# The output weights' row sums of a hybrid encoder block: three of eight formed in the opening, five spread over the first two pairs of heads

## The chip, the cores and the metric

The kernel runs on one core of one Trainium2 chip. The metric is the device time of one execution in microseconds; the figure given for a kernel is the median of its runs. A profile of one execution lies beside the times. It names the engines PE (TensorE, matmuls), PEld (its weight loads), DVE (VectorE), ACT (ScalarE), POOL (GpSimd) and SP (SyncE, which issues most DMAs).

## The reference

One layer (D = 1024) over 1024 frames with 16 learned meta tokens ahead of them. Four heads of an mLSTM matrix memory and four of multi-scale retention share one input projection; each head's output is normalised, multiplied by a gate, and all of them go through w_out. A gated MLP with a depthwise convolution and a final norm follow. All of it is float32.

```python
proj = up @ w_in                      # q, k, v, o, gates i and f of 4 mLSTM heads; q, k, v, g of 4 retention heads
qk = silu(causal_dwconv(concat(ml_q, ml_k), ml_conv_w))
h_ml = sigmoid(ml_o) * head_norm(mlstm_chunkwise(q, k, v, li, lf), ml_norm_g)
h_rt = silu(rt_g) * head_norm(retention_chunkwise(rotary(rq), rotary(rk), rv), rt_norm_g)
h = h + concat(h_ml, h_rt) @ w_out    # w_out: 2048 x 1024
h = h + (silu(causal_dwconv(u @ w_up, ffn_conv_w)) * (u @ w_gate)) @ w_down
```

## The kernel before

Every float32 product is made of three matmuls on split operands: ScalarE casts a high part ("hi", line 488), VectorE subtracts it to get the low part ("lo", line 494), and TensorE sums hi x hi, hi x lo and lo x hi (lines 948 to 950). The large products are blocked 2 x 2 and take seven block products for eight. These need sums and differences of the blocks, of activations (`usum`, lines 2046 and 2048) and of weights (lines 582 to 589). A projection of one head and kind (`wino_fm`: q and k as "q", the two gate blocks as "o"; `v_steps`: values of a pair) is seven steps over two chunks of tokens, each ended by an eviction from PSUM on ScalarE or VectorE (`evac`, lines 1039 to 1043), which the tiles `raw`, `sig` and `v` take.

**The output product** (`Seven`, from about 500 us on) also needs weight sums. For each k of eight, rows k and k + 8 of w_out (128 x 1024 each) give two combined tiles in DRAM, named `wsw65_k` and `wsw73_k`. They are formed by DMAs alone in `w_sums` (line 662): SP issues three plain copies for a k (line 667: 512 KB and twice 256 KB), and GpSimd then issues four accumulating transfers of 256 KB in three steps (`add`, line 650: two that add other quarters of w_out, then one that adds a half of the 65 tile to its other half, then one that adds that to the 73 tile). Each add has to wait until the transfers before it on the same tile have landed, and GpSimd's queue is in order, so what stands behind an add waits with it. Before the change all eight k are formed in one go in the opening: 24 copies, held until the low parts of the third token range are made (`norm_lows(2)`, line 2015), and 32 adds, step by step over all k. They are read first in the output product at 668.9 us.

**The opening** (lines 1931 to 2090) loads and norms the tokens, projects values, gates and q, k of head 4 (a retention head, handled first), and forms the activations' block sums S1 to S4. SP's loads of weights, of the rotary tables (`A<-rot`, lines 1175 and 1176) and the sums' copies share one queue in program order. From there on `go` writes the work out: the projection's steps in order, and between them pieces of side work, above all the scan of the head before. `scan_a` makes scores `s`, their weighted form `pt` (VectorE, lines 1640 and 1647), its split `ph` and `pl` (GpSimd, lines 1632 and 1651) and the weighted keys `kw` (ScalarE, line 1627); `scan_v` splits the values (`vh`, `vl`, GpSimd, lines 1663 and 1664); `scan_b` uses these on TensorE (`u` and `n`, lines 1670 to 1697). The heads come as 4, then the pairs (0, 1), (2, 3), (5, 6), then 7; a pair is the projections q a, values, o a, q b, o b.

**What sets the order.** `watch` adds up a cost for every instruction as the program is written, so that the writer has a clock per engine and for the DMA wire. A generator that is started by `spawn` is taken up again by `tick` when that clock allows; `lag(8)` lets 8 us of the planned TensorE time pass. Units in the list `units` are started when the projection steps come near them; a unit of size 0 is side work at that place. `RULES` holds seven numbers per projection (lines 48 to 69): how many units ahead pending work may be taken, how long after its planned end a step may follow, two limits on how far VectorE may run behind, the most side tasks in one slot, which of three orders of the queues is used, and how many tasks with TensorE work fit in a slot. `pinned` keeps the order so written on TensorE, VectorE and ScalarE; `last["pace"]` is the latest eviction made by VectorE.

Of the kernel before, what the change touches and what calls it, by code (L numbers as in the profile page):

```python
# [30 lines left out]
HB = 4 * P  # L31
# [15 lines left out]

RULE = (3, 0.5, 3.0, 2.5, 2, 0, 1)
RULES = {
# [39 lines left out]
def body(ctx, tc, h_in, vecs, cst, mask_in, rot, w_v0, w_vp, w_g, w_out, w_up, w_gate, w_down, out):  # L89
    nc = tc.nc  # L90
# [9 lines left out]
    def dep(later, first, sync):  # L100
        kind = mybir.DependencyClass.Sync if sync else mybir.DependencyClass.NoSync
        tc.add_manual_dep(later.ins, first.ins.name, mybir.DependencyInfo(kind, mybir.DependencyReason.DATA), reason="order")
# [4 lines left out]
    last = {}  # L107
# [194 lines left out]
    def unit(key, size, make):  # L302
        units.append((key, size, make))
# [23 lines left out]
    def main_job(nm, *srcs):  # L327
        i = job(nm, *srcs)
        line.append(i)
        return i  # L330
# [61 lines left out]
    def spawn(g, q=pend, key=None):  # L392
        if dealt[0]:
            if next(g, pend) is not pend:
                q.append(g)
                until[id(g)] = fin[0]
                owner[id(g)] = key
        elif held:
            next(g)
            held[0].append(g)  # L400
        else:
            for _ in g:
                pass
# [42 lines left out]
    def lag(us):  # L446
        t = load["PE"]
        while dealt[0] and not rush[0] and load["PE"] - t < us:
            yield
# [24 lines left out]
    class Ready(dict):  # L474
        def add(self, key):
            self[key] = fin[0] + 0.05
# [73 lines left out]
    def u_load(key, *srcs):  # L550
        nm = "_".join(str(k) for k in key)
        i = main_job(nm, *srcs)

        def make():
            r = pairs_of(nm, 2)

            def g():
                yield from jwait(i)
                yield from parts(key, r, jget(i))
                jfree(i)  # L560
            spawn(g(), key=key)
            return r
        unit(key, 2, make)
# [34 lines left out]
    def u_fm(kind, h, *extra):  # L598
        w = w_g[GI[kind, h]]
        nm = f"{kind}{h}"  # L600
        ja = main_job(nm + "a", w[:, HB:3 * HB])
        jb = main_job(nm + "b", w[:, 3 * HB:], w[:, :HB])
        quartered((kind, h), (ja, ja, jb, jb), lambda: [jraw[x][:, i * HB:(i + 1) * HB] if x in jraw else None for x in (ja, jb) for i in (0, 1)], 1, {5: (jb,), 6: (ja,)}, nm)
        for e in extra:
            e()
# [25 lines left out]
    def m_unit(h):  # L631
# [12 lines left out]
            spawn(g())  # L644
        unit(("m", h), 0, make)

    sums = {(g, st_, k): dram.tile([P, 2 * HB], F32, name=f"ws{g}{st_}_{k}") for g, n in (("w", 8), ("d", KD)) for st_ in ("65", "73") for k in range(n)}

    def add(x, y):
# [2 lines left out]
    def wsum(g, k):  # L652
# [6 lines left out]
        add(d73[:, HB:], v11)  # L659
        add(d65[:, :HB], d65[:, HB:])  # L660
        add(d73[:, :HB], d65[:, :HB])

    def w_sums(ks):
        for k in ks:
            d65, d73 = (sums["w", x, k] for x in ("65", "73"))
            for x, y in ((d65, w_out[k]), (d73[:, HB:], w_out[k][:, HB:]), (d73[:, :HB], w_out[k + 8][:, :HB])):
                dep(nc.sync.dma_start(x, y), last["lows", 2], True)
        for step in range(3):
            for k in ks:
                d65, d73 = (sums["w", x, k] for x in ("65", "73"))  # L670
                if step == 0:
                    add(d65[:, HB:], w_out[k + 8][:, HB:])
                    add(d73[:, HB:], w_out[k][:, :HB])
                else:
                    add((d65, d73)[step - 1][:, :HB], (d65[:, HB:], d65[:, :HB])[step - 1])

    dcount = [0]

# [30 lines left out]
    def r_units(*ks):  # L709
        return [lambda k=k: first_right(k) for k in ks]  # L710
# [30 lines left out]
    def v_units(p, s):  # L741
        return [lambda: v_unit(p, s)]

    q4 = w_g[GI["q", 4]]
    u_load(("q4", 0), q4[:, HB:3 * HB])
    u_load(("q4", 1), q4[:, 3 * HB:], q4[:, :HB])

    def m_units(h):
        return [lambda: m_unit(h)]
    u_fm("o", 4, *v_units(0, 0))  # L750
    prev = 4
    for p, (a, b) in enumerate(PAIRS):
        u_fm("q", a)
        u_vp(p)
        u_fm("o", a, *v_units(p, 1), *m_units(prev))
        u_fm("q", b, *(r_units(0, 1) if p == 2 else ()))
        u_fm("o", b, *(v_units(p + 1, 0) if p < 2 else r_units(2, 3)), *m_units(a))
        prev = b
    u_fm("q", 7, *r_units(4, 5))
    u_fm("v", 7, *r_units(6, 7))  # L760
# [1224 lines left out]
    w = [ready["q4", i] for i in range(2)]  # L1985
# [29 lines left out]
    norm_lows(2)  # L2015
    fourth = norm_sums(3, True)
    last["third"] = last["added"]
    w_sums(range(8))
    meta_done()
    for i, x in enumerate(x0):  # L2020
        after(V.tensor_copy(ug[:, 4 * i:4 * i + 4], x[:, :, :META]), last["third"])
# [85 lines left out]
    for p, (a, b) in enumerate(PAIRS):  # L2107
# [38 lines left out]
        prev = b  # L2146
# [14 lines left out]
    for k in range(KW):  # L2161
        if k % 2 == 0:
            x = upool.tile([P, 2 * T], F32R, tag=("uh0", "ul0", "uh1", "ul1")[k // 2], name=f"wone{k}")
        o = (k % 2) * 2 * HB
# [167 lines left out]
    for t, (st, k) in enumerate(mixw.steps):  # L2332
# [4 lines left out]
        if st == "65" and k == 5:  # L2337
            x = fp.tile([P, 4 * XW], F32, name="wm", tag="xl6", bufs=1)
# [243 lines left out]
    for i in range(1, NPAIR):  # L2582
        u, g = up_part(i), gate_part(i)
# [109 lines left out]
    for p in (1, 2):  # L2693
# [5 lines left out]
        else:  # L2699
            for mb in (1, 4):  # L2700
                x = RES[mb][:, OP[2][0]:OP[2][1]]
# [109 lines left out]
```

## Time and profile before

| what | value |
|---|---|
| median of 3 runs | 1505.08 us (1505.03 to 1505.53) |
| the profiled execution | 1503.68 us |
| its span | 1501.9 us |
| mean granted TensorE clock | 0.993 |
| moved by DMA | 223.85 MB, mean 149 GB/s |
| GpSimd's DMAs (queue q0) | 31.46 MB, 11.2% of 16 engines' span |

The span is what the trace covers; the execution's own time is 1.8 us longer. A group of the profile has its line, engine, operation, tile written and tiles read (buffer numbers left out), shape and count. "Idle before" is the time in which an engine stood still just ahead of an instruction, with the event that ended it. In the window rows the granted clock is 1.00 at full speed.

### The profile page before, as it was taken

To read this page: it belongs to the slowest core of one execution; us is meant where nothing else is said; L and a number is where in the kernel's file an instruction comes from. 1 tells how busy PE (TensorE), PEld (TensorE's weight loads), DVE (VectorE), ACT (ScalarE), POOL (GpSimd) and SP (SyncE) were. 2 spreads that over 40 slices of the span, in tenths; PEclk is the share of its full clock that TensorE was granted. 3 is DMA by queue.
4 is the path that set the end of the run, shared out by engine and by line. 5 is a ranking of instruction groups with operands and counts; after the bars stand their busy time and mean duration, and the time that the engine had idled before them with its cause. 6 is when DMAs were issued, how large, how long until landed. Compare 5 with 4: busy or idle time off the path is not lost.

```text
span 1501.9 us, 26232 instructions
## 1 busy us (share of the span) xinstructions
PE 1475.5 (98%) x10032; PEld 1342.3 (89%) x10032; DVE 1092.0 (73%) x2110; ACT 755.8 (50%) x1468; POOL 216.9 (14%) x440
## 2 busy tenths in 40 slices
PE   9988999999999999999999999999999999999997
PEld 7977999999999999987888999888888888888887
DVE  7975876778777677857867887666666666777666
ACT  6554655654655455544454664444444444444443
POOL 1233130314031403040000002222210000000000
PEclk9999999999999999999999999999999999999998
DMA  7993233223312235697333258888762225933213
GB/s 264 277 201 86 85 113 113 86 85 103 123 57 100 71 127 179 201 404 257 106 105 130 96 175 214 214 218 204 185 154 80 73 78 188 351 102 101 99 43 113
DMA packets 98014, 223.85 MB, mean 149 GB/s; under 512 B 10728, under 2 KB 25776, under 8 KB 97584
## 3 DMA queue, kind: packets, MB, share of 16 engines
q1 hardware_dynamic: 78640, 183.29, 36.1%
q0 software_dynamic: 13056, 31.46, 11.2%
q10 hardware_dynamic: 6192, 7.41, 1.4%
q8 instruction: 79, 1.29, 0.4%
q14 instruction: 47, 0.39, 0.1%
HBM read 186.44 MB, written 75.54 MB: 174 GB/s over the span
## 4 chain that ended last, share of the span: by engine, by line
PE 90%; DVE 6%; DMA 2%; ACT 1%; issue 1%; SPq 0%; DVEq 0%; POOL 0%; POOLq 0%; ACTq 0%
PE pdx L950 3%; PE pdx L949 3%; PE pdx L948 3%; PE pup_x L949 3%; PE pup_x L948 3%; PE pup_x L950 3%; PE pga_x L948 2%; PE pga_x L949 2%; PE pga_x L950 2%; PE pdy L950 2%; PE pdy L949 2%; PE pwx L950 2%; PE pdy L948 2%; PE pwx L948 2%; PE pwx L949 2%; PE n L1697 2%
## 5 line engine op out<-in xcount | busy, mean ns | idle before, releaser
L787 ACT CAST hi_up<-raw_up 128x512 fp32r<-128x512 f32 (+1 forms) x52 | 36.4, 719 | 110.1 <-PE pga_z L949 61.1
L788 DVE TENSOR_TENSOR lo_up<-raw_up,hi_up 128x512 fp32r<-128x512 f32 (+1 forms) x52 | 41.4, 810 | 38.3 <-ACT hi_up L787 37.5
L949 PE MATMUL pup_x<-ul_g,hi_up 128*128 128x256 f32 (+1 forms) x240 | 67.4, 282 | 0.0
L948 PE MATMUL pup_x<-uh_g,hi_up 128*128 128x256 f32 (+1 forms) x240 | 67.2, 282 | 0.0
L788 DVE TENSOR_TENSOR lo_ga<-fraw_ga,hi_ga 128x512 fp32r<-128x512 f32 (+1 forms) x51 | 40.6, 800 | 35.7 <-ACT hi_ga L787 35.5
L950 PE MATMUL pup_x<-uh_g,lo_up 128*128 128x256 f32 (+1 forms) x240 | 66.4, 282 | 0.0
L788 DVE TENSOR_TENSOR lo_d<-rd,hi_d 128x1024 fp32r<-128x1024 f32 (+1 forms) x34 | 37.7, 1113 | 32.8 <-ACT hi_d L787 32.7
L950 PE MATMUL pdx<-uh_d,lo_d 128*128 128x512 f32 (+1 forms) x156 | 57.9, 375 | 0.0
L787 ACT CAST hi_ga<-fraw_ga 128x512 fp32r<-128x512 f32 (+1 forms) x51 | 35.4, 712 | 44.5 <-PE pup_z L949 22.6
L949 PE MATMUL pdx<-ul_d,hi_d 128*128 128x512 f32 (+1 forms) x156 | 57.8, 374 | 0.0
L787 ACT CAST hi_d<-rd 128x1024 fp32r<-128x1024 f32 (+1 forms) x34 | 32.3, 959 | 49.1 <-PE pdy L949 32.5
L2678 POOL TENSOR_TENSOR resid<-resid,Rc 128x256 f32<-128x256 f32 x2 | 1.4, 716 | 381.4 <-ACT Rc L858 381.4
L657 POOL DMA_DIRECT2D wsd<-w_down_d x33 | 19.1, 687 | 236.5 <-DVE s2up L2436 232.8
L950 PE MATMUL pdy<-uh_d,lo_d 128*128 128x512 f32 x132 | 51.9, 393 | 0.0
L949 PE MATMUL pdy<-ul_d,hi_d 128*128 128x512 f32 x132 | 51.7, 392 | 0.0
L948 PE MATMUL pdx<-uh_d,hi_d 128*128 128x512 f32 (+1 forms) x156 | 48.5, 372 | 0.0
L948 PE MATMUL pdy<-uh_d,hi_d 128*128 128x512 f32 x132 | 47.9, 389 | 0.0
L1664 POOL TENSOR_TENSOR vl<-v,vh 128x258 fp32r<-128x258 f32 (+1 forms) x48 | 34.7, 723 | 89.2 <-PE n L1671 63.8
L948 PE MATMUL pga_x<-uh_g,hi_ga 128*128 128x512 f32 x120 | 47.5, 396 | 0.0
L949 PE MATMUL pga_x<-ul_g,hi_ga 128*128 128x512 f32 x120 | 47.5, 396 | 0.0
L950 PE MATMUL pga_x<-uh_g,lo_ga 128*128 128x512 f32 x120 | 47.1, 393 | 0.0
L949 PEld LDWEIGHTS pup_x<-ul_g,hi_up 128*128 128x128 f32 x240 | 45.4, 189 | 0.9 <-DVE ul_g L2206 0.2
(1749 smaller groups left out, 6001.1 us busy)
## 6 DMA issues: line engine op xcount, KB each, us to landing
raw_up<-w_up_d SPq DMA_DIRECT2D x22, 512.0 KB
fraw_ga<-w_gate_d SPq DMA_DIRECT2D x22, 512.0 KB
acts<-cv SPq DMA_DIRECT2D x44, 256.0 KB
wsd<-w_down_d POOLq DMA_DIRECT2D x44, 256.0 KB, 6.1
rd<-wsd SPq DMA_DIRECT2D x22, 512.0 KB
raw_m<-w_out_d SPq DMA_DIRECT2D x14, 512.0 KB
raw_vm<-w_vp_d SPq DMA_DIRECT2D x12, 512.0 KB
raw_vp<-w_vp_d SPq DMA_DIRECT2D x12, 512.0 KB
```

The lines of the kernel that those rows point to most:

```text
L657: dep(G.dma_start(x, y), last["pace"], True)
L787: AC.copy(hi[:, o:o + n], x)
L788: V.tensor_tensor(lo[:, o:o + n], x, hi[:, o:o + n].bitcast(F32), ALU.subtract)
L948: m.append(PE.matmul(pt, ah, xh_, start=first and k == 0, stop=False, skip_group_check=True))
L949: PE.matmul(pt, ah, xl_, start=False, stop=False, skip_group_check=True)
L950: m.append(PE.matmul(pt, al, xh_, start=False, stop=last and k == n - 1, skip_group_check=True))
L1664: G.tensor_tensor(low, v, vh.bitcast(F32), ALU.subtract)
L1697: PE.matmul(pn[:L, :nv], qd, state["C"][:, :nv], start=False, stop=True)
L2678: nc.gpsimd.tensor_tensor(RES[mb][:, a0:t1], RES[mb][:, a0:t1], R[1], ALU.mult)
```

## The change

Rows 0 to 2 stay in the opening, with the same copies and adds, but the copies are now held until `last["scale"]`, the scaling of the third token range, which is written before its low parts. Rows 3 to 7 become units of their own (`w_unit`): the three copies are issued when the unit is started, then each of the three steps of adds after another `lag(8)`; every one of these DMAs also waits for the eviction that `last["pace"]` names at that moment. One unit hangs on each of: o of head 0, q and o of head 1 (rows 3, 4, 5), o of head 2, q of head 3 (rows 6, 7). Four entries of `RULES` have new numbers: o of heads 0 and 1, q of heads 1 and 2.

```diff
-    ('o', 0): (4, 0.8, 3.0, 3.0, 4, 0, 1),
-    ('o', 1): (3, 1.2, 2.0, 1.5, 2, 1, 3),
+    ('o', 0): (2, 0.8, 3.0, 3.0, 1, 0, 1),
+    ('o', 1): (3, 1.2, 2.0, 1.5, 2, 1, 1),
...
+    def w_copies(k, gate):
+        d65, d73 = (sums["w", x, k] for x in ("65", "73"))
+        for x, y in ((d65, w_out[k]), (d73[:, HB:], w_out[k][:, HB:]), (d73[:, :HB], w_out[k + 8][:, :HB])):
+            dep(nc.sync.dma_start(x, y), gate, True)
+
+    def w_adds(k, step):
+        d65, d73 = (sums["w", x, k] for x in ("65", "73"))
+        if step == 0:
+            return add(d65[:, HB:], w_out[k + 8][:, HB:]), add(d73[:, HB:], w_out[k][:, :HB])
+        return add((d65, d73)[step - 1][:, :HB], (d65[:, HB:], d65[:, :HB])[step - 1]),
+
+    def w_unit(k):
+        def make():
+            def g():
+                w_copies(k, last["pace"])
+                for step in range(3):
+                    yield from lag(8)
+                    for m in w_adds(k, step):
+                        dep(m, last["pace"], True)
+            spawn(g())
+        unit(("w", k), 0, make)
...
-        u_fm("o", a, *v_units(p, 1), *m_units(prev))
-        u_fm("q", b, *(r_units(0, 1) if p == 2 else ()))
-        u_fm("o", b, *(v_units(p + 1, 0) if p < 2 else r_units(2, 3)), *m_units(a))
+        u_fm("o", a, *v_units(p, 1), *m_units(prev), *w_units(1))
+        u_fm("q", b, *(r_units(0, 1) if p == 2 else ()), *w_units(1))
+        u_fm("o", b, *(v_units(p + 1, 0) if p < 2 else r_units(2, 3)), *m_units(a), *w_units(p < 2))
...
-    w_sums(range(8))
+    for k in range(3):
+        w_copies(k, last["scale"])
+    for step in range(3):
+        for k in range(3):
+            w_adds(k, step)
```

The same instructions are there in both kernels; the change moves them. TensorE's order is the same up to the S1 step of head 0's o projection and again from the S2 step of the second pair's values on (but for a few matmuls of the 73 step of the output product, which stand in another order). Between those the scan of heads 0 and 1 stands one step later or several steps earlier among the projections' steps.

The first place is GpSimd's queue at the end of the opening, before. `wsw65_6` and the like are the sums of row 6, `ph4_1` and `pl4_1` the split scores of head 4's chunk 1.

```order
L650 DMA wsw65_6_165<-wsw65_6_165 128x512
L650 DMA wsw73_3_170<-wsw65_3_162 128x512
L650 DMA wsw65_7_166<-wsw65_7_166 128x512
L650 DMA wsw73_4_171<-wsw65_4_163 128x512
L650 DMA wsw73_5_172<-wsw65_5_164 128x512
L650 DMA wsw73_6_173<-wsw65_6_165 128x512
L650 DMA wsw73_7_174<-wsw65_7_166 128x512
L1113 MEMSET v0_10_1924 128x4x2
L1113 MEMSET v0_00_1727 128x4x2
L1632 CAST ph4_1_1397<-pt4_1_1387 128x128
```

The same place after the change.

```order
L672 DMA wsw73_0_167<-wsw65_0_159 128x512
L672 DMA wsw65_2_161<-wsw65_2_161 128x512
L672 DMA wsw73_1_168<-wsw65_1_160 128x512
L672 DMA wsw73_2_169<-wsw65_2_161 128x512
L1125 MEMSET v0_10_1889 128x4x2
L1125 MEMSET v0_00_1692 128x4x2
L1644 CAST ph4_1_1362<-pt4_1_1352 128x128
```

Twelve adds stand ahead of the cast now, where 32 stood.

The second place is VectorE's order where the rotary tables are first used, before. `uS4l` is a low part of the activations' block sum S4, `A1_4` and `A2_4` are the tables, `qT4` and `kT4` what is made of them.

```order
L1043 TENSOR_TENSOR sig_110<-sig_110,po4y1_976 128x256
L2057 TENSOR_TENSOR uS4l_929<-s4_0_838,uS4h_928 128x1056
L2057 TENSOR_TENSOR uS4l_929<-s4_1_839,uS4h_928 128x1056
L1252 TENSOR_TENSOR qT4_1018<-rawq_102,A1_4_906 128x528
L1253 TENSOR_TENSOR kT4_1019<-kT4_1019,A2_4_907 128x528
```

And after.

```order
L1055 TENSOR_TENSOR sig_110<-sig_110,po4y1_941 128x256
L1264 TENSOR_TENSOR qT4_983<-rawq_102,A1_4_871 128x528
L2073 TENSOR_TENSOR uS4l_894<-s4_0_803,uS4h_893 128x1056
L2073 TENSOR_TENSOR uS4l_894<-s4_1_804,uS4h_893 128x1056
L1265 TENSOR_TENSOR kT4_984<-kT4_984,A2_4_872 128x528
```

The product with the first table now stands ahead of the two splits.

The third place is GpSimd's queue in the scan of head 0, before, around the splits of chunk 6 (`vh0_6`, `ph0_6`, `vl0_6`, `pl0_6`).

```order
L1663 CAST vh0_6_2547<-v0_01_2250 128x258
L1710 COPY den0_2156<-v0_00_1727 128x1
L1632 CAST ph0_6_2559<-pt0_6_2553 128x128
L1664 TENSOR_TENSOR vl0_6_2548<-v0_01_2250,vh0_6_2547 128x258
L1651 TENSOR_TENSOR pl0_6_2560<-pt0_6_2553,ph0_6_2559 128x128
```

And after.

```order
L1675 CAST vh0_6_2529<-v0_01_2215 128x258
L1722 COPY den0_2121<-v0_00_1692 128x1
L672 DMA wsw65_3_162<-w_out_d 128x512
L672 DMA wsw73_3_170<-w_out_d 128x512
L1644 CAST ph0_6_2541<-pt0_6_2535 128x128
L1676 TENSOR_TENSOR vl0_6_2530<-v0_01_2215,vh0_6_2529 128x258
L1663 TENSOR_TENSOR pl0_6_2542<-pt0_6_2535,ph0_6_2541 128x128
```

The first two adds of row 3 stand ahead of the split of chunk 6's scores; the other rows' adds stand in the same way among the splits of heads 0 to 3, the four of row 4 and the four of row 7 each in one piece ahead of the first split of heads 1 and 3. In SP's order, row 3's copies stand between the two loads for head 1's q, row 4's ahead of the first load for head 1's o, row 5's ahead of the first load for head 2's q (`raw_q2a`), and rows 6 and 7 likewise in the second pair.

More of the change, by code (lines that the diff above doesn't have):

```diff
@@ L661, in wsum @@
         add(d73[:, :HB], d65[:, :HB])
[L663 to L675, printed above, removed]
     dcount = [0]
@@ L746, in body, with w_units @@
     u_load(("q4", 1), q4[:, 3 * HB:], q4[:, :HB])
+    wk_ = list(range(3, 8))
+    def w_units(n):
+        return [lambda: wk_ and w_unit(wk_.pop(0))] * n
     def m_units(h):
```

4 rows, old and new, of the table RULES are left out of this document.

## The prediction

> **What bounds the kernel now.** I read the page first (busy shares, the chain of waits), then busy time by stage, then TensorE's own waits, and last the timelines of the two stretches where TensorE stands still.
>
> ```profile
> PE 1475.5 (98%) x10032; PEld 1342.3 (89%) x10032; DVE 1092.0 (73%) x2110; ACT 755.8 (50%) x1468; POOL 216.9 (14%) x440
> 80.00:100.00 20.00, 14.72 (x107) 14.04 (x106) 16.85 (x49) 10.38 (x18) 7.21 (x10) 0.91 0.99 203
> 100.00:120.00 20.00, 14.05 (x107) 12.33 (x106) 11.13 (x29) 9.02 (x23) 7.20 (x10) 0.94 0.98 177
> 140.00:550.00 410.00, 409.72 (x3389) 392.59 (x3389) 302.98 (x698) 230.62 (x482) 89.95 (x223) 1.00 0.29 94
> ```
>
> The window rows give the stretch, its length, busy time of PE, PEld, DVE, ACT and POOL, the granted TensorE clock, the DMA engines' busy share and GB/s. TensorE is busy 98% of the span, so time can only be won where it stands. Of its 26 us idle, 5.3 + 6.0 = 11.2 us lie between 80 and 120 us, where the DMA engines are at 0.98 to 0.99; from 140 to 550 us, where the five moved rows go, it stands 0.28 us and DMA is at 0.29. The first two of its waits make nearly all of the 11.2:
>
> ```profile
> PE n L1670 <- POOL ph L1632: 6.8, 1, 6.8
> PE po4x L948 <- ACT sig L1041: 4.6, 1, 4.6
> PE pz L1879 <- POOL zero L289: 1.3, 1, 1.3
> PE prc L854 <- DVE rcolc L845: 0.6, 1, 0.6
> ```
>
> (Engine, tile and line that waited, its releaser, total us, times, longest. The third comes before the first matmul.) I take the two in turn, with the change's part in each.
>
> **Term 1, the wait of 4.6 us.** TensorE needs an eviction that ScalarE makes late, since ScalarE stands behind a rotary copy that waits for VectorE, and VectorE waits for the rotary tables:
>
> ```profile
> 68.71 0.34 SPq L1175 DMA_DIRECT2D A<-rot_d  x1
> 69.88 13.06 DMA A<-rot_d
> 74.54 2.42 DVE L2057 TENSOR_TENSOR uS4l<-s,uS4h 128x1056 fp32r<-128x1056 f32 x2
> 80.35 0.71 DVE L1252 TENSOR_TENSOR qT<-rawq,A 128x528 f32<-128x528 f32 x1 [3.39 <-DMA A<-rot_d]
> 83.03 0.71 DVE L1253 TENSOR_TENSOR kT<-kT,A 128x528 f32<-128x528 f32 x1 [1.97 <-DMA A<-rot_d]
> 81.15 0.63 ACT L1249 COPY rawq<-rawk 64x528 f32<-64x528 f32 x1 [3.83 <-DVE qT L1252]
> 86.16 0.36 ACT L1041 ACTIVATE sig<-po4x 128x256 f32<-128x256 f32 x1
> 86.57 0.39 PE L948 MATMUL po4x<-uS3h,hi_o 128*128 128x256 f32 x1 [4.64 <-ACT sig L1041]
> 89.62 0.42 PE L948 MATMUL po4y<-uS4h,hi_o 128*128 128x258 f32 x1
> 89.83 0.42 PE L949 MATMUL po4y<-uS4l,hi_o 128*128 128x258 f32 x1
> 93.55 0.28 PE L948 MATMUL po4x<-u22h,hi_o 128*128 128x256 f32 x1
> 93.67 0.28 PE L949 MATMUL po4x<-u22l,hi_o 128*128 128x256 f32 x1
> 254.78 0.62 ACT L488 CAST hi_q<-raw_q2a 128x512 fp32r<-128x512 f32 x1 [0.41 <-DMA raw_q2a<-w_g_d]
> 251.05 0.33 SPq L338 DMA_DIRECT2D raw_q2a<-w_g_d  x1
> ```
>
> The second table took 13.06 us from its issue. A load of nearly the same size in a quiet stretch, raw_q2a, took 254.78 - 251.05 = 3.73 us. The queue is full because of the sums:
>
> ```profile
> 26.43 1.56 DVE x L916 x4
> 32.63 30.92 SPq L667 DMA_DIRECT2D wsw<-w_out_d  x24
> L650 POOL DMA_DIRECT2D wsw<-w_out_d x16: 805/814/960, 37.2 to 95.9; - x16
> L650 POOL DMA_DIRECT2D wsw<-wsw x16: 812/822/837, 49.3 to 120.0; - x16
> DMA to landing us min/median/max: 4.3/7.6/12.0
> ```
>
> The change leaves 9 of 24 copies (8 MB in 30.92 us, so 3 MB in about 11.6) and 12 of 32 adds, and the copies wait for the last scaling in the first row instead of the split that ends at 32.6. From 28.0 us that is copies to 40 and three steps of adds at 4.3 to 7.6 us each, over by 53 to 63 us, before the tables are asked for at 68.7. Those stay where they are: they wait for a buffer. The tables then land at about 72.4 and 75, and VectorE loses neither 3.39 nor 1.97: its work comes 5.36 us earlier. ScalarE's eviction goes from 86.16 to 80.8, before TensorE asks for it at 81.9. The stall of 4.64 goes, and with it the slow matmuls behind it: from 86.57 to about 90.2 they start 0.21 us apart where the pair at 93.55 starts 0.12 apart, 1.65 us lost. TensorE would win 6.3, but the next steps wait for VectorE's sums, which come only 5.36 earlier, so **5.4 us** (bounds 3, if the tables still land late, and 6.3). The order puts the first table product ahead of two splits; by 74.5 (the place of the splits now) its table has landed, so that costs nothing; TensorE comes to those splits only after 81.9, so a table that is some us late is covered too.
>
> **Term 2, the wait of 6.8 us.** The first matmul on chunk 1's split scores waits for GpSimd, whose in-order queue holds the adds, to the last:
>
> ```profile
> 114.15 0.28 PE L1672 MATMUL u<-vh,kl 128*128 128x256 f32 x1
> 111.54 0.40 SPq L338 DMA_DIRECT2D raw_vp<-w_vp_d  x1
> 117.70 1.14 ACT L488 CAST hi_vp<-raw_vp 128x512 fp32r<-128x512 f32 x2 [5.13 <-DMA raw_vp<-w_vp_d]
> 118.75 0.36 ACT L1627 ACTIVATE kw<-s,cs 128x128 fp32r<-128x128 f32 x1
> 119.97 0.82 POOL L650 DMA_DIRECT2D wsw<-wsw  x1 [5.13 <-issue]
> 120.89 0.29 POOL L1632 CAST ph<-pt 128x128 fp32r<-128x128 f32 x1
> 121.24 0.58 PE L1670 MATMUL n<-vh,ph 128*128 128x256 f32 x1 [6.81 <-POOL ph L1632]
> 124.54 0.30 PE L949 MATMUL pq0x<-uS3l,hi_q 128*128 128x264 f32 x1
> ```
>
> With no add behind 63 us GpSimd is free and this cast follows its input at once. The stall goes, and so does a second slow stretch of 3.3 us at half pace (121.24 to 124.54), about 1.65 us: 8.5 us. What is late next is the same cast for chunk 2. It needs kw at 118.75, which stands on ScalarE behind two casts that wait for raw_vp. That load, 5.4 us earlier (106.1) and 3.73 us long, lands at 109.9; the casts end at 111.0, kw at 111.4, the scores' split some 1.3 us later, 112.7. TensorE, 5.4 us earlier and unstalled, comes for it at about 111.7 (114.3 - 5.4, then 1.0 of chunk 1, 1.5 of projection, 0.3 of scores). So 1 us stays (0 to 2.4, the upper end with the 6.1 us that the load took before): **7.5 us**, bounds 6 and 8.5.
>
> The trace has no stall of TensorE between 0.6 and 4.6 us but the 1.3 before its first matmul, so whether this remaining 1 us slows the matmuls after it isn't shown; the nearest row, the 4.64 us, would add 1.65, the 0.6 nothing, and I take the short one, being nearer. The Trainium skill (TensorE: Matmul & The Clock Gate, "What's actually happening") says that the clock halves only after an idle window of about 3.4 us; by it the residue costs no clock and the sum stays, by the long row it would be 1.65 us less.
>
> **Term 3, the five rows in the pairs.** Each adds three copies to SP's queue (median 0.49 us) and four adds of about 0.82 us to GpSimd, which is busy 90 of 410 us there: 20 x 0.82 = 16 us fit. Neither engine is on the path; what counts is who stands behind them. On GpSimd that is the splits of scores and values:
>
> ```profile
> 203.16 0.29 POOL L1632 CAST ph<-pt 128x128 fp32r<-128x128 f32 x1 [2.27 <-DVE pt L1640]
> 205.36 0.47 POOL L1651 TENSOR_TENSOR pl<-pt,ph 128x128 fp32r<-128x128 f32 x1
> 208.51 0.29 PE L1670 MATMUL n<-vh,ph 128*128 128x258 f32 x1
> 213.82 0.29 POOL L1632 CAST ph<-pt 128x128 fp32r<-128x128 f32 x1 [3.11 <-DVE pt L1640]
> L948 PE MATMUL pq2x<-u11h,hi_o x8: 283/285/393, 265.2 to 267.9; 128*128 128x264 f32 x8
> ```
>
> Ahead of the two casts GpSimd stood 2.27 and 3.11 us, and the split of the first ends (205.83) 2.7 us before its matmul: two adds of 1.6 us are covered if their operands have landed. They mostly have: the plan lets 8 us of TensorE's time pass between a row's steps, and the adds here land in 7.6 us at the median in a full queue. On SP a row's megabyte takes 30.92 / 8 = 3.9 us of the queue and stands ahead of a weight load (row 5's ahead of raw_q2a). That load's cast was already 0.41 us late; but TensorE uses it only at 265.2, 10 us later. The copies' and adds' wait for a VectorE eviction holds back the same splits, which wait for later VectorE results anyway. The new order rules alter TensorE's row from head 0's o steps to the first steps of the second value projection, with equal work; the trace cannot price that. I bound term 3 by 0, as all has cover and there is no idle to win (0.28 us), and by 6, one stall like the 4.64 with its slow stretch; nearer the cover: **1.5 us**.
>
> **The sum.** The profiled execution took 1503.68 us, its span 1501.9. 1503.68 - 5.4 - 7.5 + 1.5 = 1492.3. The median of the runs, 1505.08, is 1.4 above that execution, so the forecast is 1493.7. The bounds of the terms: gains of 3 + 6 - 6 = 3 up to 6.3 + 8.5 = 14.8, that is 1502.1 to 1490.3.
>
> **The rivals.**
>
> *Only GpSimd's stall goes (0.13).* The copies start earlier, beside the opening's weight loads, and the tables or VectorE stay as late as now. For it: VectorE is busy 16.85 of 20 us from 80 to 100. Against: 5.36 us of its idle time there name the tables. Gain 7.5 - 1.5 = 6: 1499.
>
> *Loads stand behind copies (0.08).* In the pairs three loads (of q1, o1 and q2) follow a row's copies in SP's order; if each cast holds ScalarE for the 3.9 us and TensorE feels it whole, 11.7 us come back of 12.9: 1503.9, no change. Against it stand the 10 us of raw_q2a. The Trainium skill (DMA: Bandwidth & Descriptors, "Queues, rings and completion order") says that a DMA engine takes the descriptors of one issuing queue in order, which is this mechanism and speaks against the change; the 13.06 us of the table bear it out in a full queue.
>
> *GpSimd blocks the scan (0.10, slower).* An add at the head of GpSimd's queue waits for its transfer, as at 119.97, and the splits behind it stand. If each of five rows held GpSimd for the median landing of 7.6 us with 2.7 of slack, TensorE would stall 4.9 us a row, 24.5 in all: 1505.1 - 12.9 + 24.5 = 1516.7. It turns the sign once a row costs over 12.9 / 5 = 2.6 us, so where GpSimd is held over 5.3 us a row. Against it: the 8 us between steps.
>
> **Chances.** Forecast 0.69, the three rivals 0.13, 0.08 and 0.10. A difference of 0.2%, 3 us, is about what a measurement of this kernel tells from none. Faster by more: the forecast and the first rival, 0.82. Within it: the second, 0.08. Slower: 0.10. The range takes the bounds of the terms and the first rival, widened at the low end by a microsecond for the runs' own spread: 1489 to 1502. It leaves out the second and third rivals.
>
> **What would show it.** Right: the rotary product without a DMA wait and TensorE's wait on that eviction under 1 us; no add later than about 63 us until the pairs; the split for chunk 1 right behind its scores; the projection's matmul that stands at 124.54 now about 12 us earlier; in the pairs at most 2 us of idle. Wrong: tables that still take over 8 us; a wait for the chunk 2 split above 2.4 us; adds in the pairs that hold GpSimd over 5 us with TensorE standing behind them.

## The result, and the profile after

The changed kernel takes 1495.59 us (median of 6 runs, 1493.04 to 1498.06) beside 1505.05 (6 runs, 1502.08 to 1505.53): a ratio of 0.9939, 95% interval 0.9926 to 0.9953, or 9.5 us less. The forecast was 1493.7. The profiled execution took 1498.06 us (span 1496.3), the slowest of the six, so its trace shows only 1498.06 - 1503.68 = -5.6 us; which steps make that can be read from it one by one.

The stages and waits first (windows and TensorE's own waits of the changed kernel, columns as before):

```profile
80.00:100.00 20.00, 18.09 (x146) 17.12 (x145) 17.86 (x53) 12.05 (x24) 0.00 (x0) 1.00 0.09 28
100.00:120.00 20.00, 18.08 (x136) 16.36 (x135) 12.93 (x39) 7.70 (x20) 6.47 (x16) 1.00 0.32 108
140.00:550.00 410.00, 406.21 (x3350) 387.59 (x3349) 306.37 (x689) 227.00 (x476) 111.20 (x237) 1.00 0.43 121
...
PE s L1622 <- DVE kl L1648: 3.5, 2, 1.9
PE pz L1891 <- POOL zero L289: 1.3, 1, 1.3
PE po4x L960 <- DVE sig L1055: 0.8, 1, 0.8
```

Between 80 and 120 us TensorE stands 3.8 us in place of 11.2, at full clock, and the DMA engines are at 0.09 and 0.32 in place of 0.99 and 0.98. Both large waits are gone. But from 140 to 550 us, where it stood 0.28 us, it now stands 3.8.

To price each stretch, five matmuls are looked up in both traces: the time of one before minus its time after is the lead that the changed kernel has there. First the rows of before, then the same matmuls after:

```profile
59.16 0.65 PE L988 MATMUL pv<-w0lo,u22h 128*128 128x264 f32 x4
104.84 0.29 PE L949 MATMUL pq0x<-uS2l,hi_q 128*128 128x264 f32 x1
192.17 0.28 PE L950 MATMUL po0y<-u12h,lo_o 128*128 128x258 f32 x1
331.15 0.28 PE L949 MATMUL pv1y<-lo_vp,uS4h 128*128 128x256 f32 x1
449.95 0.29 PE L950 MATMUL pq5x<-u22h,lo_q 128*128 128x264 f32 x1
```

```profile
60.35 0.65 PE L1000 MATMUL pv<-w0lo,u22h 128*128 128x264 f32 x4
100.73 0.29 PE L961 MATMUL pq0x<-uS2l,hi_q 128*128 128x264 f32 x1
181.28 0.28 PE L962 MATMUL po0y<-u12h,lo_o 128*128 128x258 f32 x1
323.27 0.28 PE L961 MATMUL pv1y<-lo_vp,uS4h 128*128 128x256 f32 x1
444.29 0.29 PE L962 MATMUL pq5x<-u22h,lo_q 128*128 128x264 f32 x1
```

The lead is -1.19, 4.11, 10.89, 7.88 and 5.66 us. So the opening loses 1.2, the stretch of the rotary tables wins 5.3, the stretch of the first scan wins 6.8, and the pairs give back 3.0 and then 2.2, 5.2 together. After that nothing changes (5.62 at the end).

The two places of the gain, as the timelines of GpSimd, SP, VectorE, ScalarE and TensorE have them (start, duration, instruction, idle time before it and its cause):

```profile
59.76 0.83 POOL L672 DMA_DIRECT2D wsw<-wsw  x1 [2.55 <-DMA wsw<-wsw]
69.29 0.34 SPq L1187 DMA_DIRECT2D A<-rot_d  x1
75.12 0.70 DVE L1264 TENSOR_TENSOR qT<-rawq,A 128x528 f32<-128x528 f32 x1
82.06 0.36 ACT L1053 ACTIVATE sig<-po4x 128x256 f32<-128x256 f32 x1
108.62 0.29 POOL L1644 CAST ph<-pt 128x128 fp32r<-128x128 f32 x1
111.80 0.28 PE L961 MATMUL pq0x<-uS3l,hi_q 128*128 128x264 f32 x1
112.02 1.14 ACT L488 CAST hi_vp<-raw_vp 128x512 fp32r<-128x512 f32 x2 [3.55 <-DMA raw_vp<-w_vp_d]
114.12 0.49 PE L1622 MATMUL s<-qT,kT 128*128 128x128 f32 x2 [1.55 <-DVE kl L1648]
```

The last add of the opening is issued at 59.76 us, VectorE's product needs the table at 75.12 and does not wait, and the eviction that came at 86.16 comes at 82.06. Chunk 1's split starts at 108.62 us, 0.9 us after its input, behind a small fill that waits for a transfer of the gates; TensorE does not stand for it. The projection's matmul that stood at 124.54 stands at 111.80, 12.7 us earlier. What is late next is chunk 2, as forecast, behind ScalarE's casts that wait for `raw_vp`. TensorE stands 1.55 us, but ahead of the next scores and for VectorE's `kl` (the low part of the weighted keys), not for the split that the forecast named.

The 1.2 us lost in the opening are no wait. The granted clock (the third figure from the end of a window row) halves for some 3.4 us, which costs 1.35 us; up to there the lead is +0.16:

```profile
36.00:37.00 1.00, 1.00 (x9) 1.00 (x8) 0.91 (x3) 0.94 (x2) 0.21 (x1) 0.80 1.17 377
38.00:39.00 1.00, 1.00 (x7) 1.00 (x6) 0.26 (x1) 0.61 (x2) 0.00 (x0) 0.50 0.97 223
40.00:41.00 1.00, 1.00 (x10) 1.00 (x10) 1.00 (x4) 0.50 (x1) 0.00 (x0) 1.00 1.12 207
```

### The profile page after: what moved, and what is told of

Read it like the earlier page. It is cut to its first block, busy times and chain, and to the rows that moved or that the text cites. A ratio compares the mean times of both kernels' runs of the same rounds, so it can differ in the third digit from the quotient of the medians.

```text
span 1496.3 us, 26258 instructions
## 1 busy us (share of the span) xinstructions
PE 1475.4 (99%) x10032; PEld 1340.2 (90%) x10032; DVE 1096.4 (73%) x2110; ACT 756.2 (51%) x1469; POOL 224.1 (15%) x440
## 3 DMA queue, kind: packets, MB, share of 16 engines
q1 hardware_dynamic: 78640, 183.29, 36.2%
q0 software_dynamic: 13056, 31.46, 11.6%
## 4 chain that ended last, share of the span: by engine, by line
PE 84%; DVE 5%; DMA 2%; ACT 1%; issue 1%; DVEq 0%; ACTq 0%; SPq 0%
PE pdx L962 3%; PE pdx L961 3%; PE pdx L960 3%; PE pup_x L961 3%; PE pup_x L960 3%; PE pup_x L962 3%; PE pga_x L960 3%; PE pga_x L961 2%; PE pga_x L962 2%; PE pdy L962 2%; PE pdy L961 2%; PE pwx L962 2%; PE pdy L960 2%; PE pwx L960 2%; PE pwx L961 2%; PE n L1709 2%
```

## The experiments

Each kernel is read in the same way: its lead over the trace of before at the same five matmuls, and the difference from one to the next. The last two columns are stretches, named by what lies there in the change. The ratio is to runs of the kernel before that were taken beside it (medians 1504.22 to 1505.59 us).

| kernel | median us | ratio to before (95%) | opening | tables | scan | rows 3 to 6 | row 7 |
|---|---|---|---|---|---|---|---|
| the change | 1495.59 | 0.9939 (0.9926 to 0.9953) | -1.19 | +5.30 | +6.78 | -3.01 | -2.22 |
| pairs_none | 1489.94 | 0.9894 (0.9881 to 0.9906) | +1.80 | +4.71 | +7.92 | -1.08 | -0.02 |
| pairs_copies | 1490.45 | 0.9904 (0.9886 to 0.9922) | +0.35 | +5.33 | +7.95 | -1.45 | 0.00 |
| rules_only | 1507.19 | 1.0008 (0.9999 to 1.0016) | +1.83 | +0.86 | -2.42 | -1.31 | 0.00 |
| rules_old | 1499.70 | 0.9963 (0.9951 to 0.9975) | +1.88 | +4.75 | +8.09 | -8.36 | -3.86 |
| late7 | 1497.00 | 0.9936 (0.9924 to 0.9949) | +0.33 | +5.32 | +7.89 | -2.99 | +0.02 |
| gate_only | 1500.56 | 0.9973 (0.9962 to 0.9984) | -1.30 | +5.30 | -1.39 | 0.00 | 0.00 |
| sp_copies | 1511.31 | 1.0044 (1.0027 to 1.0062) | -1.35 | -14.09 | +7.68 | 0.00 | +0.02 |
| four_four | 1495.27 | 0.9933 (0.9913 to 0.9952) | -1.79 | +3.99 | +7.62 | -2.83 | -0.01 |
| window2 | 1494.58 | 0.9940 (0.9920 to 0.9959) | +1.87 | +4.71 | +5.69 | -2.97 | +0.01 |
| spread2 | 1500.82 | 0.9982 (0.9971 to 0.9993) | +0.25 | +4.71 | -1.23 | -2.60 | -0.01 |
| spread4 | 1520.55 | 1.0115 (1.0098 to 1.0131) | +0.33 | +5.33 | -20.79 | -1.34 | +0.02 |
| window2_early | 1493.29 | 0.9930 (0.9914 to 0.9945) | -1.37 | +5.09 | +8.64 | -2.09 | -0.02 |

Each lead is that of one execution. The opening column differs by up to 3.7 us among the kernels, and by 3.0 among three whose opening is the same instruction by instruction (the change, pairs_none, late7): it holds the first loads and that half clock, and no verdict rests on it. Between the change and late7, which are alike up to the fourth mark, the scan column differs by 1.11 us and the column of rows 3 to 6 by 0.02.

**pairs_none: the five rows left out.**

```diff
-    wk_ = list(range(3, 8))
+    wk_ = []
...
+    for k in range(3, 8):
+        sums["w", "65", k] = sums["w", "73", k] = w_out[k]
```

> The changed kernel without the five paced rows: neither copies nor adds for rows 3 to 7, whose steps of the output projection read the weights themselves in place of their sums (so those sums are left out). TensorE's row is that of the changed kernel, word for word. By the matmuls' times in the two profiles the changed kernel wins 5.3 us up to 86 us and 6.8 up to 125 us, and gives back 3.0 between 205 and 315 us and 2.2 at 417 us. Theory A (the rows' transfers make all that is given back): 1495.6 - 5.2 = 1490.4, no idle of TensorE above 0.5 us between 140 and 550. Theory B (the new order rules make the 3.0, the rows only the 2.2 at 417 us): 1493.4, with 1.6 us of idle left between 200 and 315. Theory C (the rows cost nothing, the losses are of the profiled execution alone): 1495.6.

1489.94 us: theory A's number, with a part of B. Without the rows 1.08 us are still lost between the third mark and the fourth, so of the 5.2 the rows' transfers make 1.9 + 2.2 = 4.1. Of the 1.08 us 0.87 are no wait: between these marks as many matmuls keep TensorE busy for 139.85 us in place of 138.98. Compared matmul by matmul with this kernel, the change loses 1.0 us at 257 to 259 us, a few us behind a late load (`raw_q2a`, see below), and 2.1 at 417; the rest, about 1 us, comes in pieces of 0.2 to 0.7 whose cause was not followed.

**rules_only and rules_old: the order rules taken apart from the rows.** The kernel before gets the four new entries of `RULES` (rules_only), the changed kernel the four old ones (rules_old, the same lines the other way round):

```diff
-    ('o', 0): (4, 0.8, 3.0, 3.0, 4, 0, 1),
+    ('o', 0): (2, 0.8, 3.0, 3.0, 1, 0, 1),
...
```

> The kernel before with the four new order rules alone. Theory A: 1505.1, the two stalls of 4.6 and 6.8 us as before, and no idle above 0.5 us between 140 and 420. Theory B (the new rules cost 3.0 us between 205 and 315 us): 1508.1. Theory C (the new rules are part of the gain): under 1502.

> The changed kernel with the four order rules of before; TensorE's row is then that of the kernel before up to the output projection. Theory A (the rows' transfers make the 3.0 us lost between 205 and 315 us; the rules are neutral): 1495.6, with stalls in that stretch at other matmuls. Theory B (the new rules make them): 1492.6. Theory C (the new rules spare a stall behind the rows' adds): over 1498, with TensorE waiting for GpSimd's splits behind adds for 2 us or more between 150 and 420.

TensorE's waits with the new rules alone, up to 140 us:

```profile
PE n L1670 <- POOL ph L1632: 7.9, 1, 7.9
PE po4x L948 <- ACT sig L1041: 3.8, 1, 3.8
```

Both stalls stay and the time does not fall: the rules are no part of the opening's gain. (The -2.42 in the scan stretch is a wait 1.1 us longer and a half clock of 10.2 us in place of 6.8, at a place where TensorE's order is still that of before.) They cost 1.31 us in the pairs, much as in pairs_none (1.08), which theory A had at nothing. With the rows and the old rules it is theory C: the pairs lose 8.36 and 3.86 us in place of 3.01 and 2.22. One of the waits, and what SP and ScalarE did ahead of it:

```profile
PE s L1622 <- DVE pt L1652: 2.9, 1, 2.9
...
239.76 0.52 SPq L338 DMA_DIRECT2D raw_q2a<-w_g_d  x1
246.65 0.62 ACT L488 CAST hi_q<-raw_q2a 128x512 fp32r<-128x512 f32 x1 [4.80 <-DMA raw_q2a<-w_g_d]
```

ScalarE stands 4.80 us for a weight load that a row's copies precede on SP; VectorE stands 3.25 us for the next cast, and its `pt`, for which TensorE waits, stands behind that. So the stall there was at a late load and not, as C had it, at a split behind an add. No add is issued between that load and 244.97 us, so it is late behind copies: 6.89 us from its issue to its cast, much as with copies alone (6.85, next run). The stalls also brought the half clock, for 6.8 us from 248.9 and 3.4 from 419.6, so some 5 of the 12.2 us lost in the pairs are that (an estimate, half of 10.2). The new rules cost a microsecond by themselves and spare 7 where the rows run (12.2 less 5.2 by the leads; 4.1 by the medians).

**pairs_copies: the paced copies without the adds.**

```diff
                 for step in range(3):
                     yield from lag(8)
-                    for m in w_adds(k, step):
-                        dep(m, last["pace"], True)
```

> The changed kernel with the 15 paced copies of rows 3 to 7 but without their 20 adds (their sums are left out). Without any of the five rows the time was 1489.9 (ratio to before 0.989), with all of them 1495.6 (0.994). Theory S (what the rows cost is that weight loads stand behind copies on SP and its queue): 1494 to 1495.6. Theory D (it is the adds, which load the DMA engines beside a weight load, as at 397 us, or hold GpSimd): 1490 to 1491, and raw_q5a lands within 6 us of its issue.

1490.45 us, theory D. By the leads the 15 copies cost 0.37 us (1.45 against 1.08), and nothing at row 7; the medians do not tell this kernel from pairs_none. The same load in the changed kernel (first) and without the adds (second):

```profile
397.21 0.82 POOL L672 DMA_DIRECT2D wsw<-wsw  x1 [7.82 <-DVE sig L1055]
397.44 0.33 SPq L338 DMA_DIRECT2D raw_q5a<-w_g_d  x1
406.00 0.62 ACT L488 CAST hi_o<-raw_q5a 128x512 fp32r<-128x512 f32 x1 [3.24 <-DMA raw_q5a<-w_g_d]
```

```profile
393.12 0.33 SPq L338 DMA_DIRECT2D raw_q5a<-w_g_d  x1
398.35 0.62 ACT L488 CAST hi_o<-raw_q5a 128x512 fp32r<-128x512 f32 x1
```

With an add issued 0.2 us ahead of it the load is there 8.56 us after its issue, and ScalarE has waited 3.24 us for it; without, the cast starts after 5.23 and waits for nothing. For raw_q2a, with an add issued 2.4 us ahead of it, it is 8.56 us with a wait of 3.29 in the changed kernel, 6.85 with 1.56 beside copies alone, and 5.17 with none in pairs_none. What an add takes of the DMA engines is seen in the queues of the changed kernel from 360 to 420 us (packets, MB, share of 16 engines):

```profile
q1 hardware_dynamic: 2480, 7.35, 37.7%
q0 software_dynamic: 864, 1.57, 20.0%
```

GpSimd's accumulating transfers hold 12.7% per MB, SP's plain ones (weight loads and copies) 5.1%: here an add holds the engines 2.5 times as long as a plain transfer of its size. Over the whole profile of before the factor is 1.8 (31.46 MB of GpSimd's in 11.2%, 183.29 MB of SP's in 36.1%).

**late7: row 7 some 100 us later.**

```diff
-        u_fm("q", b, *(r_units(0, 1) if p == 2 else ()), *w_units(1))
-        u_fm("o", b, ..., *w_units(p < 2))
+        u_fm("q", b, *(r_units(0, 1) if p == 2 else ()), *w_units(p < 1))
+        u_fm("o", b, ..., *w_units(p < 1))
```

> The changed kernel with row 7's sums hung on the unit of o5 in place of q3, some 120 us later; nothing else moves, TensorE's row is the same. Theory A (row 7's last add at 397.2 us shares the DMA engines with the load of raw_q5a, which took 8.4 us in place of 5.8, and TensorE's 1.9 us wait at 417 us is its work): 1495.6 - 2.2 = 1493.4, raw_q5a lands within 6 us of its issue and that wait is gone. Rival (the load is late by the transfers of the meta rows issued 1.7 us ahead of it, whatever the add does): 1495.6, and the wait stays.

The wait at 417 us is gone, so the row's transfers had caused it. But the time stays at 1497.0, since in this execution the row costs 4.15 us between 480 and 540 us, where its copies (at 501.5) and adds (508.6) run ahead of other loads; about 1.5 of that is the half clock from 520.4 to 523.8 us, the rest waits:

```profile
PE pm L619 <- DMA raw_m<-w_out_d: 2.7, 3, 1.7
```

**gate_only: the earlier release alone, all eight rows in the opening.**

```diff
-                dep(nc.sync.dma_start(x, y), last["lows", 2], True)
+                dep(nc.sync.dma_start(x, y), last["scale"], True)
```

> The kernel before, with its 24 opening copies released by the last scaling (as in the changed kernel, 4 us earlier) in place of the split of the third part; all eight rows stay in the opening, TensorE's row is the same up to the output projection. Theory (the gain comes from the rows that left the opening; the gate only shifts the same transfers by 4 us): the last add about 4 us earlier, so the second stall 3 to 7 us long, the first still over 3: 1501 to 1505 (ratio 0.9975 to 1.0). Rival (the earlier gate alone makes a good part of the gain): under 1500.

The time lies just under the theory's range (from 1501) and above the rival's (under 1500), and the theory's reason fails: the first stall goes entirely (+5.30, as much as in the changed kernel) and the second stays.

```profile
27.93 30.86 SPq L667 DMA_DIRECT2D wsw<-w_out_d  x24
76.39 0.70 DVE L1252 TENSOR_TENSOR qT<-rawq,A 128x528 f32<-128x528 f32 x1
PE n L1670 <- POOL ph L1632: 8.0, 1, 8.0
```

The 24 copies start 4.7 us earlier than before and their issue ends at 58.8 in place of 63.6; the tables, asked for at 69.4, are there in time although the adds still run until 118. So the first stall hung on the copies that stand ahead of the tables, not on the adds.

**sp_copies: 20 adds replaced by 20 plain copies on SP.**

```diff
+    def put(k, x, y):
+        if k < 3:
+            add(x, y)
+        else:
+            dep(nc.sync.dma_start(spare.pop(), y), last["lows", 2], True)
```

> The kernel before, with the 20 adds of rows 3 to 7 replaced by 20 plain copies of the same pieces into spare DRAM, issued by SP behind the 24 others (so the sums of five rows are left out): GpSimd issues 12 adds in place of 32, and the DMA queue stays full beyond the tables' load. Theory A (two causes: the first stall is the full DMA queue's, the second GpSimd's): the tables still land 8 us or more after their issue and the first stall stays at 3 to 7 us; the wait for chunk 1's split falls from 6.8 to under 2.5; 1505.6 - 6.8 = 1498.8. Rival D (both stalls are the full queue's): the second stays too, 1505. Rival G (both are GpSimd's): both go, 1493.5.

Theory A's first cause is there, far larger than it said, so that the time is 12.5 us over its figure:

```profile
PE po4x L956 <- ACT sig L1049: 18.9, 1, 18.9
96.58 0.71 DVE L1260 TENSOR_TENSOR qT<-rawq,A 128x528 f32<-128x528 f32 x1 [18.52 <-DMA A<-rot_d]
```

The tables' load now has 44 copies ahead of it on SP and is issued at 89.6 us, so the first stall grows from 4.6 to 18.9 us. The wait for GpSimd's split vanishes (+7.68 in that stretch), and GpSimd issues its last add at 75.95; but TensorE also comes to that split some 14 us later than before, about 128 us, when the 32 adds of before (the last at 119.97) would be over too. So this run shows the cause of the first stall, SP's queue of copies, and does not prove that of the second. That GpSimd's queue of adds makes the second rests on gate_only, where the adds and the stall stay, on the changed kernel, where both are gone, and on window2 and spread4 below.

**four_four: four rows in the opening, four in the pairs.**

```diff
-    wk_ = list(range(3, 8))
+    wk_ = list(range(4, 8))
...
-    for k in range(3):
+    for k in range(4):
```

> The changed kernel with four rows in the opening and four in the pairs (row 7 falls away from q3's unit, its sums hang where row 6's did, and so on). TensorE's row is the same. Theory: the opening's transfers, over at 62 us with three rows (34 us from 28), end at about 73; the tables, asked for at 68, come 2 to 3 us later, which their cover of VectorE's work hides in part: 0 to 1 us lost there; 2.2 us won at 417 us: 1493.9 (0.9925 of before). Rival (the opening has no room for a fourth row: tables 5 us or more late, VectorE loses it all): 1497 or more.

1495.27 us, not told apart from the change. Row 7's 2.2 us are won, and 1.3 are lost at the tables, for which VectorE waits again:

```profile
77.92 0.71 DVE L1264 TENSOR_TENSOR qT<-rawq,A 128x528 f32<-128x528 f32 x1 [2.12 <-DMA A<-rot_d]
```

The opening's room ends between three rows and four.

**window2, spread2, spread4, window2_early: rows in the idle stretch after the tables.** From 85 to 105 us the DMA engines are idle in the changed kernel, and GpSimd too up to 101. In all four kernels the first paced rows hang on the unit of o4, with a pause ahead of the copies (`wait`) and one between steps (`gap`):

```diff
-    def w_unit(k):
+    def w_unit(k, wait=0, gap=8):
         def make():
             def g():
+                yield from lag(wait)
                 w_copies(k, last["pace"])
                 for step in range(3):
-                    yield from lag(8)
+                    yield from lag(gap)
...
-    u_fm("o", 4, *v_units(0, 0))
+    u_fm("o", 4, *v_units(0, 0), *[lambda k=k: w_unit(k, 8, 3) for k in range(3, 5)])
```

> The changed kernel with rows 3 and 4 hung on the unit of o4, so that their copies go behind the load of raw_q0b at about 79 us and their adds ahead of chunk 1's split at about 107: the stretch in which the DMA engines stand idle after the tables. Rows 5 to 7 take the places of rows 3 to 5; TensorE's row is the same. Theory: 22 us of transfers fit (three rows took 34 in the opening), GpSimd is free by 105, and the pairs cost 2.2 + 0.4 us less: 1493.0 (0.992 of before). Rival (adds still hold GpSimd when the split is due, a small form of the old second stall): a wait for it of over 2 us, 1497 or more.

1494.58 us. The copies waited for the eviction that releases them until 87.7 us, so the last add came late and its split with it:

```profile
87.66 3.68 SPq L650 DMA_DIRECT2D wsw<-w_out_d  x6
109.03 0.82 POOL L673 DMA_DIRECT2D wsw<-wsw  x1 [0.91 <-DMA wsw<-wsw]
PE n L1683 <- POOL ph L1645: 2.4, 1, 2.4
```

That is the rival's mechanism at half its price: the scan's stretch wins 5.7 us, not 7.9.

With two (spread2) and four rows (spread4), and `wait` 12 and `gap` 10 in place of 8 and 3, the later adds stand among the scan's splits.

> As the kernel with rows 3 and 4 on the unit of o4, copies behind raw_q0b's load at about 79 us and the first four adds ahead of chunk 1's split; but the later adds only ahead of chunk 3's and chunk 5's splits (117 and 127 us), where the DMA engines stand idle too and the adds' operands have long landed. Rows 5 to 7 in the places of rows 3 to 5. Theory (an add costs only where a split stands behind it unlanded, or a load beside it): the 2.9 us that the earlier form lost at 107 us are not lost, the pairs still cost 1.9: 1494.6 - 2.2 = 1492.4 (0.9915 of before). Rival (any add among the scan's splits holds them): stalls of over 2 us between 107 and 140, 1495 or more.

> The same with four rows (3 to 6) on the unit of o4: copies from about 79 to 95 us, eight adds ahead of chunk 1's split, four ahead of chunk 3's, four ahead of chunk 5's; only row 7 in the pairs, at o0. Theory: without any row in the pairs the time was 1489.9; the one row there costs 0.5, and 0 to 1.5 are lost where the adds meet the loads of the second values' weights (104 to 107 us): 1490.5 to 1492 (0.990 to 0.991 of before). Rival (eight adds don't land by 105 us, or those loads come late): a wait of over 2 us for chunk 1's or chunk 2's split, 1494 or more.

Both came out on the rival's side. In spread2 (1500.82 us) TensorE waits 1.54, 1.14 and 0.48 us for GpSimd's splits; which of these the adds ahead of them make was not followed. Its longest wait, 2.68 us, is for `kl` behind ScalarE, which stands for a load issued beside the adds:

```profile
114.43 1.14 ACT L488 CAST hi_vp<-raw_vp 128x512 fp32r<-128x512 f32 x2 [6.80 <-DMA raw_vp<-w_vp_d]
```

spread4 takes 1520.55 us, far slower than before. Its GpSimd row and TensorE's wait:

```profile
99.73 0.11 POOL L1126 MEMSET v<- 128x8 f32 x1 [41.10 <-ACT gates L1357]
102.61 2.51 POOL L673 DMA_DIRECT2D wsw<-w_out_d  x3 [2.76 <-DVE rawq L1056]
123.16 0.82 POOL L673 DMA_DIRECT2D wsw<-w_out_d  x1 [1.11 <-issue]
PE n L1683 <- POOL ph L1645: 15.6, 1, 15.6
```

The pause put the first adds behind a small fill that waits for the gates until 99.7 us; GpSimd, idle for 41 us, could not take them earlier. The eight adds then end at 124, and the split behind them with them. An idle engine was no free place: its queue's order decided.

In window2_early the release is taken earlier (after 6 of the 8 us of pause; the copies start at 75.95 us in place of 87.66), which moves the copies ahead of raw_q0b and all adds ahead of the fill:

```diff
-                yield from lag(wait)
-                w_copies(k, last["pace"])
+                yield from lag(min(wait, 6))
+                gate = last["pace"]
+                yield from lag(wait - 6)
+                w_copies(k, gate if wait else last["pace"])
```

> The kernel with rows 3 and 4 on the unit of o4 once more, with the release of their copies and adds taken from an eviction some 14 us earlier: there the copies were issued at 87.7 us, ten us after the load ahead of them, and the last add at 109.0 us held the split that TensorE then waited for (2.4 us; 2.9 lost). Here the copies go right behind the loads of q0a and of the second values' weights, at about 73 us and ahead of raw_q0b, and the adds end by about 98. Theory (an add costs where a split stands behind it): no wait for chunk 1's split, the pairs still cost 1.9 with rows 5 to 7: 1494.6 - 2.4 = 1492.2, ratio 0.9915 of before. Rival (raw_q0b, now behind two rows' copies, comes after 88 us, when VectorE wants it): over 2 us lost between 88 and 100, 1494.5 or more.

```profile
75.95 4.41 SPq L650 DMA_DIRECT2D wsw<-w_out_d  x6
99.26 0.82 POOL L675 DMA_DIRECT2D wsw<-wsw  x1 [0.45 <-DMA wsw<-wsw]
101.68 0.11 POOL L1128 MEMSET v<- 128x8 f32 x1 [1.59 <-ACT gates L1359]
108.62 0.29 POOL L1647 CAST ph<-pt 128x128 fp32r<-128x128 f32 x1
```

The adds end at 100, no split waits, and the pairs lose 2.09 us, of which the rules make 1.1. With 1493.29 us it is the fastest kernel that forms all sums; its interval overlaps that of the change, so the gain over it rests on the trace: 2.09 us lost in the pairs in place of 5.2.

## Why the prediction was right or wrong

**Term 1 (5.4 forecast, 5.3 measured).** The chain from the late table over VectorE and ScalarE to TensorE was right, and so was the cap by VectorE. What it credited was too much: it put the gain down to the rows that leave the queue, and gate_only shows that the earlier release alone brings the same 5.3. The prediction named that release in the same sentence and did not price it by itself. Whether three rows would have been enough with the old release was not run. Of the full DMA queue that it blamed, SP's copies ahead of the tables mattered; GpSimd's adds did not.

**Term 2 (7.5 forecast, 6.8 measured; 7.9 in pairs_none, late7 and pairs_copies, whose opening is the same).** GpSimd's in-order queue was the cause: in gate_only all adds stay and so does the stall, in the change the last add is issued at 59.76 us and the stall is gone, and in window2 and spread4 adds ahead of the split bring 2.4 and 15.6 us of it back. The residue at chunk 2 was 1.55 us where 1 was forecast (at most 0.4 in those three), inside its bound of 2.4. It came by the forecast load, which was issued 1.3 us later than reckoned, and it cost no clock: the matmuls behind it start 0.12 us apart.

**Term 3 (1.5 forecast, 5.2 measured; bounds 0 and 6).** This is the term that was mis-sized. It consists of 1.1 us for the rules, 1.9 for rows 3 to 6 (0.4 of that the copies) and 2.2 for row 7. Two sentences of it failed. "Neither engine is on the path; what counts is who stands behind them" looked at the queues of SP and GpSimd only: the adds cost through a third party, the DMA engines, where a weight load beside an add came 1.7 and 3.3 us later than without the adds. And "TensorE uses it only at 265.2, 10 us later" took the cover of a load from TensorE's use of the weights, while its cast stands in ScalarE's row ahead of the scan's evictions. The wait of 0.41 us that the prediction quoted was the warning: that cast had no slack. On GpSimd itself the price was right: the longest that an add stood for a transfer in the pairs is this one, and TensorE's waits there name no GpSimd work. GpSimd stood up to 9.66 us ahead of an add for the VectorE eviction that releases it, longer than the 5 us named as a sign of being wrong, but TensorE did not stand behind that.

```profile
211.13 0.83 POOL L672 DMA_DIRECT2D wsw<-wsw  x1 [3.55 <-DMA wsw<-wsw]
```

**The sum.** In the profiled execution 5.3 + 6.8 - 5.2 - 1.35 (the half clock at 37 us) + 0.1 make the 5.6 us that it shows. The median of the runs is 2.5 us under that execution and so 1.9 us over the forecast; where the others of the six are faster was not seen, as they have no trace.

**The rivals.** *Only GpSimd's stall goes* is out, by the 5.3 us. *Loads stand behind copies* names the right sufferers and, in the changed kernel, the wrong offender: copies alone cost 0.4 us in the pairs. With the old order rules they cost more, as the 2.9 us of rules_old show. It is the true account of the first stall, where sp_copies shows it at full size: the tables' load is issued 20.9 us later, behind the 44 copies. The rule cited for it from the Trainium skill (DMA: Bandwidth & Descriptors, "Queues, rings and completion order") speaks of the order within a DMA engine. The 18.9 us go the same way, but no run here separates that order from the late issue on SP. *GpSimd blocks the scan* did not happen in the change, but spread4 shows that it was no idle fear: 15.6 us for eight adds at the wrong place.

**Of the signs named beforehand** all of the opening's held (no wait of the rotary product, waits for its eviction under 1 us, last add before 63, the split 0.9 us behind its input, 12.7 us at the projection's matmul). The one for the pairs, at most 2 us of idle, failed with 3.8.

## What to carry to other kernels

Price a moved transfer in two places: on the queue that issues it, for whoever stands behind it there, and on the DMA engines, for whatever load is in flight beside it; an accumulating DRAM transfer held them here about twice as long as a plain one of its size (1.8 to 2.5 times). Take the cover of a load from the first instruction that reads it, in its engine's row, and not from the engine that needs the product at last. And where one change does several things at once (an earlier release, fewer rows, new order rules), make one kernel for each: here the release alone held one of the two gains, and the rules that cost a microsecond alone spared several with the rows, part of them by sparing the half clock.

## What the runs showed of the hardware

The clock fell to half without a long stall, and not always with one. In the changed kernel it was at 0.50 from about 36.6 to 40.0 us though TensorE had stood for at most 0.45 us at a time since 20 us. Eight of the fourteen profiles show that loss of 1.3 to 1.6 us there, with the same instructions as some that do not. Behind stalls, a wait of 2.68 us in spread2 brought about 3.4 us at half clock, one of 2.86 us in rules_old about 6.8, one of 2.09 us there about 3.4, and waits of 0.64 and 1.71 us shortly after one another in late7 about 3.4; waits of 1.55 and 1.94 us (the change) and 2.4 us (window2) brought none. So the length of a single wait does not decide it. The Trainium skill (TensorE: Matmul & The Clock Gate, "What's actually happening") gives half clock as the state after at least one idle window of about 3.4 us, and calls the window free-running. The lengths of 3.4 and twice 3.4 us and the difference between like executions agree with a free-running window. If an idle window means one without any work, the rule does not agree with these waits, which are shorter, nor with the case at 37 us. What share of idle is enough stays open.
